# Joined column groups in a list scheduler, and a 64-row product run on 128 rows: a hybrid decoder layer on one Trainium2 core

## The chip, the core and the metric

The kernel runs on one core of one Trainium2 chip. The core has five engines that run their own queues of instructions: TensorE (in the profile PE for matmuls and PEld for the loads of their stationary operand), VectorE (DVE), ScalarE (ACT), GpSimd (POOL) and SyncE (SP), which here issues all DMAs. Matmuls read SBUF and write PSUM, which has eight banks. The metric is the device time of one execution in microseconds; the time of a kernel is the median of its runs.

## The reference, cut to what matters

One step of a decoder layer for two request groups: 2048 prompt tokens and 8 decode tokens, width 1024, all in float32. The layer has a parallel mixer (a Conformer convolution beside a gated DeltaNet with 4 heads), a cross-attention into 256 memory tokens, and a SwiGLU FFN of width 2816.

```python
def gated_delta_chunked(q, k, v, g, beta, s0):
    ...                                   # q, k, v, g, beta in chunks of 64 tokens
    lower = jnp.where(strict, jnp.einsum('nbhid,nbhjd->nbhij', kb, k) * decay, 0.0)
    a_mat = lower + jnp.eye(c, dtype=lower.dtype)
    u = lax.linalg.triangular_solve(a_mat, v * beta[..., None], left_side=True, lower=True, unit_diagonal=True)
    w = lax.linalg.triangular_solve(a_mat, kb * jnp.exp(gc)[..., None], left_side=True, lower=True, unit_diagonal=True)
    ...                                   # scan over the chunks with the state s

def memory_attend(h, mem_k, mem_v, w_mq, w_mo):
    q = (h @ w_mq).reshape(bsz, seq, MEM_HEADS, MEM_HD)
    s = jnp.einsum('blhd,bmhd->bhlm', q.astype(jnp.float32), mem_k.astype(jnp.float32)) * (MEM_HD ** -0.5)
    pr = jax.nn.softmax(s, axis=-1)
    o = jnp.einsum('bhlm,bmhd->blhd', pr, mem_v.astype(jnp.float32)).astype(h.dtype)
    return o.reshape(bsz, seq, MEM_HEADS * MEM_HD) @ w_mo

def decoder_layer(...):
    y, conv_buf, sc_buf, s = parallel_mixer(rms_norm(x, norm_mix), ...)
    x = x + y
    x = x + memory_attend(rms_norm(x, norm_mem_q), mem_k, mem_v, w_mq, w_mo)
    x = x + swiglu(rms_norm(x, norm_ffn), w_gate, w_up, w_down)
```

For the prompt, keys and values of the memory come from the memory tokens; each of the 8 decode rows has its own cached memory keys and values of 256 tokens.

## The kernel before, in words

The prompt is cut into four blocks of 512 tokens (`NB`, `TB`). For each pair of blocks the input projections run first; beside them run the convolution and the DeltaNet. Then come, block by block, the output projection, the memory attention and the FFN. The large products split each float32 operand into two parts of a shorter type and add three products (`three`), so that weights pass through a split on ACT and on DVE or POOL (tiles `w` out of `raw`). In the trace, `hd`, `glua` and `glub` are the input projections, `mkv`, `wk` and `vp` the memory's products, `rg` and `sc` the output projection and the memory attention, `fx`, `fy`, `fz` and `dn`, `dx`, `dy`, `dz` the FFN.

**The DeltaNet's inverse.** `dn_front` (lines 1795 to 1948) makes, for one head and one block of 512 tokens, the inverse of the lower triangular matrix; there are 4 x 4 = 16 such fronts. It works in four chunks of 128 tokens. `base_inverse` inverts the diagonal blocks of 16 rows on DVE and POOL; the result goes through DRAM (`zw`, `zt_`) into two tiles: `Tm`, and `W`, which first has 64 rows. Then blocks are joined, from 16 to 32 rows, from 32 to 64, and from 64 to 128. A step for `s` in (16, 32) is, in lines 1911 to 1932: four products of `lt` (or of its odd blocks, `lo`) and `Tm` into `pu1`; a multiplication with a mask on DVE into `u1`; four products of `W` and `u1` into `pu2`; an addition into `Tm` on DVE; four transposes of `Tm`, which ACT copies into a new `W` of 128 rows. In the step with s = 16 the second product runs on 64 rows (`W` has 64, and `u1[:n]` with n = 64), in the step with s = 32 on 128. Each of the four products is float32 and shows as two instructions, so a group of four shows as x8: `pu<-u,W 64*128` in the first step, `pu<-u,W 128*128` in the second. `u1` is one constant tile for all fronts; a front takes it with `held_l`, so one front uses it at a time.

`W`, `Tm` and most other working tiles come from one pool of 28 tiles (`t2`, `NT2`). Its users include the fronts' operands, the convolution's, the blocks of x, and the decode rows' operands.

**The decode rows' column groups.** `quad` (line 664) is a matmul whose stationary operand has at most 32 columns and whose result lies in PSUM rows 32j to 32j + 31. Four such products with j = 0 to 3 stand one after another in a loop at two places:

```python
                for (d, mc), vt in vts.items():                                       # line 2527, dec_attend
                    quad(po, 2 * d + mc, pbs[mc][:, (b + d) * 32 : (b + d + 1) * 32], vt, b == 0, b == DEC - 2)
        for j in range(4):                                                            # line 2433, dec_rows
            quad(at[0], j, h[:, k0 + j, :], wts[j], k0 == 0, k0 == 4)
```

The first is the product of probabilities and cached values of the decode rows (tile `podd`, moving operand `vtd`, 8 groups of four). The second is the decode rows' two projections `w_mq` and `w_mo` (tile `dr`, moving operand `raw`, 8 groups of four). Here too each product shows as two instructions.

**What sets the order.** The program is written down twice. First, generators ("lanes") and the main path issue operations in the order in which a simple clock finds them due; nothing is emitted yet, each goes onto a tape (`Tape.add`) with a modelled cost (`Tape.cost`). Then a list scheduler (`Tape.order`, lines 301 to 507) makes each engine's final order. `Tape.graph` finds which operations must come before which (`preds`). `Tape.keys` gives each a key: for PE its place on the tape; for other engines the smallest key among those that need its result or its tile next, but at most 300 (`LATER`) behind its own place. An engine that comes free takes, among the operations whose predecessors are done by the model's clock, the one with the smallest key. An operation whose tile isn't given yet also takes a buffer of its pool then; it may do so ahead of earlier users of the pool as long as the counts of live tiles leave room (`may`). Additions, subtractions and multiplications in SBUF may go to DVE or to POOL, whichever the scheduler finds better (`other`). So a change of a modelled cost, or one operation more, can change the order of everything behind it. The costs that bear on the change:

```python
            if args[1].dtype == F32 and m <= 32 and n >= 256:
                return n * 0.4492 + 15, False, None
```

and, for a fill on POOL, `40 + 0.85 * n` ns for n elements in a row.

Of the kernel before, what the change touches and what calls it, by code (L numbers as in the profile page):

```python
# [8 lines left out]
F32 = mybir.dt.float32  # L9
# [5 lines left out]
P = 128  # L15
# [5 lines left out]
NT = TB // P  # L21
# [133 lines left out]
class Tape:  # L155
# [10 lines left out]

    def __init__(self):
        self.ops, self.tag_of, self.bufs, self.psum = [], {}, {}, set()
        self.real, self.other, self.given = {}, {}, {}

    def pool(self, pool, bufs, psum=False):
        return TapePool(self, pool, bufs, psum)
# [16 lines left out]
    def cost(self, eng, op, args, kw, outs, ins):  # L189

        n = max(elems(a) for a in outs + ins) if ins else elems(outs[0])
        psum_in = any(a.name in self.psum for a in ins)
        if eng == "pe":
            m = elems(args[1])
            n = elems(args[2])
            if op == "transpose":
                return max(n, m) * 0.835 + 3, False, None
            if args[1].dtype == F32 and m <= 32 and n >= 256:
                return n * 0.4492 + 15, False, None
            if args[1].dtype == F32:  # L200
                return 2 * (max(max(m, 64) * 0.835, 2 * n * 0.4492) + 3), False, None
            return max(max(m, 64) * 0.835, (n if n >= 256 else 4 * n) * 0.4492) + 3, False, None
        if eng == "sp":
            size = 4
            for x in outs[0].shape:
                size *= x
            return max(size / 295.0, 90.0), False, None
        if eng == "act":
            ptr = len(ins) - 1
            return 0.834 * n + (50 if psum_in else 94) + 93 * ptr + (92 if "accum_out" in kw else 0), False, SETS.get(kw.get("func"))  # L210
        big = sum(a.name not in self.psum and elems(a) > 1 for a in ins)
        if eng == "dve":
            ptr = any(hasattr(kw.get(k), "shape") for k in ("scalar", "scalar1"))
            half = op in ("tensor_copy", "tensor_scalar") and not psum_in
            shared = big > 1 or (half and n > 2 and not any(a.name in self.psum for a in outs))
            return 68 + (61 if ptr else 0) + n * (6.2 if op == "reciprocal" else 0.525 if half else 1.042), shared, None
        if kw.get("op") == ALU.pow:
            return 280 + 180 * n, True, None
        if op in ("memset", "affine_select"):
            return 40 + 0.85 * n, False, None  # L220
        return 150 + n * (2.15 if op == "tensor_tensor" else 3.4), True, None

    def box(self, a):

# [20 lines left out]
    def graph(self):  # L245

        writes, reads, last_pe = {}, {}, {}
        preds, tiles = [], []
        over = lambda x, y: x[0] <= y[1] and y[0] <= x[1] and x[2] <= y[3] and y[2] <= x[3]
        inside = lambda x, y: y[0] <= x[0] and x[1] <= y[1] and y[2] <= x[2] and x[3] <= y[3]  # L250
        for n, (eng, op, _, args, _, outs, ins, _) in enumerate(self.ops):
            p = {}
            for a in ins:
                if a.name in self.tag_of:
                    b = self.box(a)
                    for k, x in writes.get(a.name, ()):
                        if over(b, x):
                            p[k] = 1
            for a in outs:
                if a.name in self.tag_of:  # L260
                    b = self.box(a)
                    for k, x in writes.get(a.name, ()):
                        if over(b, x):
                            p[k] = 1
                    for k, x in reads.get(a.name, ()):
                        if over(b, x):
                            p[k] = 1
                    if eng == "pe":
                        if a.name in last_pe:
                            p[last_pe[a.name]] = 1  # L270
                        last_pe[a.name] = n
            for a in outs:
                if a.name in self.tag_of:
                    b = self.box(a)
                    for d in (writes, reads):
                        d[a.name] = [(k, x) for k, x in d.get(a.name, ()) if not inside(x, b)]
                    writes[a.name].append((n, b))
            for a in ins:
                if a.name in self.tag_of:
                    reads.setdefault(a.name, []).append((n, self.box(a)))  # L280
            p.pop(n, None)
            preds.append(list(p))
            tiles.append(list(dict.fromkeys(a.name for a in outs + ins if a.name in self.tag_of)))
        return preds, tiles

    def keys(self, succs, line, first, tiles):


        N = len(self.ops)
        nxt = {}  # L290
        for tag, ts in line.items():
            for k, t in enumerate(ts[: -self.bufs[tag]]):
                nxt[t] = first[ts[k + self.bufs[tag]]]
        key = list(range(N))
        for n in range(N - 1, -1, -1):
            if self.ops[n][0] != "pe":
                after = [key[m] for m in succs[n]] + [key[nxt[t]] for t in tiles[n] if t in nxt and nxt[t] > n]
                key[n] = min([n + LATER, *after])
        return key

    def order(self):
# [336 lines left out]
def hybrid_step(ctx: ExitStack, tc: tile.TileContext, i: dict, o: list):  # L638
# [8 lines left out]
    def dma(out, in_, after=0.0):  # L647
        SP.dma_start(out=out, in_=in_)
        n = 4
        for x in out.shape:  # L650
            n *= x
        C.at["sp"] = max(C.at["sp"] + 60, C.when([in_]), after)
        C.at["dma"] = max(C.at["dma"], C.at["sp"] + 1100) + max(n / 360.0, 60.0)
        C.ready[out.name] = max(C.ready.get(out.name, 0.0), C.at["dma"] + 1650)
        C.used[in_.name] = max(C.used.get(in_.name, 0.0), C.at["dma"])

    def mm(out, lhsT, rhs, start, stop, skip=False):
        n = elems(rhs)
        four = lhsT.dtype == F32 or n < 256
        S.wait(max(C.when([lhsT, rhs]), C.ready.get("free " + out.name, 0.0) if start else 0.0))  # L660
        PE.matmul(out, lhsT, rhs, start=start, stop=stop, skip_group_check=skip)
        C.run("pe", 3 + max(n, 64) * (4 if four else 1) / 2.4, [lhsT, rhs], out, 90.0)
# [34 lines left out]
    def t2(name, shape=(P, TB), dt=F32):  # L697
        n = 1
        for x in shape[1:]:
            n *= x  # L700
        t = t2pool.tile([P, W2], dt, tag="t2", name=nm(name))
        live["t2"].add(t.name)
        assert len(live["t2"]) <= NT2, sorted(live["t2"])
        v = t[: shape[0], :n]
        if len(shape) == 3:
            v = v.rearrange("p (a b) -> p a b", a=shape[1])
        return v
# [34 lines left out]
    def const(name, shape, dt=F32):  # L742
        return cst.tile(list(shape), dt, tag=name, name=name)
# [1003 lines left out]
    def z_odd(z):  # L1747

        f = z.rearrange("a b -> (a b)").rearrange("(c x) -> c x", c=NT)
        return f[:, 0 : 64 * P].rearrange("c (r i) -> r c i", i=P)  # L1750
# [44 lines left out]
    def dn_front(h, b, sc, prev, out):  # L1795
# [96 lines left out]
        drop(bit, du)  # L1892
        held_x.pop()
        held_w.pop()
        W = t2("W", (64, NT, P))
        dma(W, z_odd(zw[z]))
        Tm = t2("Tm", (P, NT, P))
        dma(Tm, z_full(zt_[z]))
        yield lambda: prev is None or "done" in prev
# [11 lines left out]
        for s in LEV[:-1]:  # L1911
            n = nms[s].shape[0]
            yield ("ps", "s")
            pu = ps("pu1", shape=(n, NT, 64))
            for c in range(NT):
                mm(pu[:, c, :], (lo if n == 64 else lt)[:, c, :], left(Tm, s)[:, c], True, True)
            V.tensor_tensor(out=u1[:n], in0=pu, in1=bc(nms[s], 1, [n, NT, 64]), op=ALU.mult)
            yield u1
            yield ("ps", "s")
            pu = ps("pu2", shape=(P, NT, 64))  # L1920
            for c in range(NT):
                mm(pu[:, c, :], W[:, c, :], u1[:n, c, :], True, True)
            V.tensor_tensor(out=left(Tm, s), in0=pu.rearrange("p c (b s) -> p c b s", s=s), in1=left(Tm, s), op=ALU.add)
            yield Tm
            yield ("ps", "s")
            pt = ps("ptw", shape=(P, NT, P))
            for c in range(NT):
                transpose(pt[:, c, :], Tm[:, c, :], ident)
            drop(W)
            W = t2("W", (P, NT, P))  # L1930
            A.activation(out=W, in_=pt, func=AF.Copy)
            yield W
# [216 lines left out]
    drop(zt)  # L2149

    u1s = [const("u1", [P, NT, 64])]
    S.add(dec_start())
    fr_ = {(b, h): {} for b in range(NB) for h in range(H)}
    ch_ = {(b, h): {} for b in range(NB) for h in range(H)}
# [976 lines left out]
```

## Time and profile before

| what | us |
|---|---|
| median of 3 runs (lowest to highest) | 2936.22 (2935.59 to 2937.78) |
| the profiled execution's own time | 2932.24 |
| its span, first to last instruction | 2930.5 |
| PE busy in the span | 2890.9 |
| DVE busy | 2470.0 |
| ACT busy | 1452.0 |
| POOL busy | 754.0 |

The span is what the trace covers; the execution's own time also holds what lies around it. A row of a group of instructions reads: line, engine, operation, output <- inputs, shapes (for a matmul the active rows and columns of the stationary operand, then the moving operand), count; then busy time and mean length of one; then the engine's idle time ahead of them and what ended it. Line L515 is the place where the tape issues everything, so groups are told apart by tile names. A row of the timeline has the start, the time from start to end, and the merged instructions. A row by windows has the window, its length, and for each engine its busy time and number of instructions, then the granted TensorE clock, the share of the DMA engines and GB/s.

### The profile page before, as it was taken

The page shows a single profiled execution, that of the slowest core. Times are in us where ns is not written, and L with a number is a line of the kernel's source. Part 1 is how long each engine was busy: PE and PEld are TensorE (multiplying, and loading weights), DVE is VectorE, ACT ScalarE, POOL GpSimd, SP SyncE. Part 2 cuts the span into 40 slices and gives each one's busy share as a digit, 9 for nine tenths or more (in the row PEclk, how much of TensorE's full clock was granted, in tenths as well). Part 3 has the DMA queues.
Part 4 walks back from the last instruction along what each step waited for, and adds up shares of the span by engine and source line. Part 5 has one row for each costly group of instructions (what it writes and reads, how often), then busy time and mean ns, then how long its engine had stood idle before and what let it go on. Part 6 is the DMA issues. An engine that isn't in the chain of part 4 may idle for free.

```text
span 2930.5 us, 55769 instructions
## 1 busy us (share of the span) xinstructions
PE 2890.9 (99%) x19620; PEld 2598.0 (89%) x19620; DVE 2470.0 (84%) x5364; ACT 1452.0 (50%) x3034; POOL 754.0 (26%) x850
## 2 busy tenths in 40 slices
PE   9999999999999999999999999999999999999998
PEld 8999878888888887989888789999888999999998
DVE  8868988999978897978888877788867888888888
ACT  7544545555664445545454443344444444444444
POOL 3211342553313034613201810000542232410000
PEclk9999999999999999999999999999999999999999
DMA  6533435777774334866677767777636666666664
GB/s 222 155 97 105 128 115 162 228 247 258 225 243 124 119 102 133 261 192 201 213 259 251 246 217 246 232 232 238 201 102 207 210 214 199 209 230 197 214 209 131
DMA packets 363032, 569.40 MB, mean 194 GB/s; under 512 B 55840, under 2 KB 158560, under 8 KB 362736
## 3 DMA queue, kind: packets, MB, share of 16 engines
q1 hardware_dynamic: 362752, 565.84, 60.3%
q8 instruction: 155, 2.54, 0.3%
q14 instruction: 125, 1.02, 0.1%
HBM read 457.77 MB, written 108.51 MB: 193 GB/s over the span
## 4 chain that ended last, share of the span: by engine, by line
PE 51%; DVE 2%; DMA 2%; ACT 1%; issue 1%; POOL 0%; SPq 0%; POOLq 0%; DVEq 0%; ACTq 0%
PE fy L515 11%; PE fz L515 8%; PE fx L515 7%; PE rg L515 6%; PE dx L515 5%; PE dn L515 5%; PE dz L515 3%; PE sc L515 3%; PE dy L515 1%; DMA w<-sums 1%; DVE w L515 1%; PE pu L515 0%; PE podd L515 0%; DVE x L515 0%; PE pch L515 0%
## 5 line engine op out<-in xcount | busy, mean ns | idle before, releaser
L515 ACT ACTIVATE w<-raw 128x512 fp32r<-128x512 f32 (+1 forms) x1066 | 649.5, 619 | 888.9 <-issue 138.2
L515 DVE TENSOR_TENSOR w<-raw,w 128x512 fp32r<-128x512 f32 (+1 forms) x861 | 610.8, 713 | 161.5 <-ACT w L515 156.8
L515 PE MATMUL fy<-op,w 128*128 128x256 f32 (+1 forms) x3168 | 434.3, 282 | 0.1
L515 PEld LDWEIGHTS fy<-op,w 128*128 128x128 f32 x3168 | 399.1, 188 | 7.6 <-issue 1.8
L515 PE MATMUL hd<-hT,w 128*128 128x512 f32 (+2 forms) x1920 | 394.2, 356 | 1.0 <-DVE hT L515 0.5
L515 POOL TENSOR_TENSOR w<-raw,w 128x512 fp32r<-128x512 f32 (+1 forms) x205 | 282.5, 1382 | 341.7 <-ACT w L515 277.9
L515 DVE SCALAR_TENSOR_TENSOR cacc<-cu,cw,cacc 128x512 f32<-128x512 f32 x480 | 357.6, 745 | 9.2 <-ACT cacc L515 5.7
L515 PEld LDWEIGHTS hd<-hT,w 128*128 128x128 f32 x1920 | 302.6, 188 | 45.4 <-ACT w L515 1.2
L515 PE MATMUL fx<-op,w 128*128 128x256 f32 (+1 forms) x2112 | 297.3, 283 | 0.3
L515 PE MATMUL fz<-op,w 128*128 128x256 f32 (+1 forms) x2112 | 285.8, 283 | 1.8 <-DMA w<-sums 1.7
L515 PEld LDWEIGHTS fx<-op,w 128*128 128x128 f32 x2112 | 269.4, 189 | 8.3 <-ACT w L515 3.4
L515 PEld LDWEIGHTS fz<-op,w 128*128 128x128 f32 x2112 | 264.5, 188 | 9.0 <-issue 4.8
L515 PE MATMUL dx<-fo,w 128*128 128x256 f32 (+1 forms) x1344 | 197.8, 283 | 0.7 <-DVE x L515 0.6
L515 PE MATMUL rg<-pT,w 128*128 128x512 f32 x768 | 191.3, 400 | 2.1 <-ACT pr L515 0.9
L515 PE MATMUL dn<-ff,w 128*128 128x512 f32 (+2 forms) x960 | 192.0, 353 | 0.3 <-ACT ffs L515 0.2
L515 PE MATMUL sc<-w,hT 128*128 128x512 f32 x768 | 188.5, 399 | 3.6 <-ACT pr L515 3.6
L515 PE MATMUL rg<-catS,w 128*128 128x512 f32 (+2 forms) x960 | 186.2, 351 | 0.0
L515 PEld LDWEIGHTS dx<-fo,w 128*128 128x128 f32 x1344 | 174.7, 188 | 2.7 <-DVE x L515 1.3
L515 PEld LDWEIGHTS rg<-catS,w 128*128 128x128 f32 x960 | 154.6, 188 | 24.6
L515 PEld LDWEIGHTS sc<-w,hT 128*128 128x128 f32 x768 | 141.4, 188 | 36.8 <-ACT pr L515 5.9
L515 PEld LDWEIGHTS rg<-pT,w 128*128 128x128 f32 x768 | 140.5, 188 | 35.8 <-ACT pr L515 2.2
L515 PEld LDWEIGHTS dn<-ff,w 128*128 128x128 f32 x960 | 150.9, 188 | 22.0 <-DVE ffs L515 0.5
(421 smaller groups left out, 4836.6 us busy)
## 6 DMA issues: line engine op xcount, KB each, us to landing
w<-sums SPq DMA_DIRECT2D x222, 512.0 KB, 4.4
raw<-in_w_gate_dram SPq DMA_DIRECT2D x192, 256.0 KB, 3.5
sums<-w SPq DMA_DIRECT2D x66, 512.0 KB, 3.7
raw<-in_w_up_dram SPq DMA_DIRECT2D x118, 256.0 KB, 3.4
raw<-in_w_down_dram SPq DMA_DIRECT2D x224, 128.0 KB, 2.8
raw<-in_w_in_dram SPq DMA_DIRECT2D x96, 256.0 KB, 3.2
raw<-sums SPq DMA_DIRECT2D x74, 256.0 KB, 3.3
raw<-wk SPq DMA_DIRECT2D x64, 256.0 KB, 2.8
```

The costliest lines, as they stand in the source:

```text
L515: fn(*args, **kw)
```

## The change: two edits

**First edit, the list scheduler.** A new method `quarter` names a float32 matmul with at most 32 stationary columns and 256 or more moving ones. Its modelled cost goes from 0.4492 n + 15 to 0.4492 n + 38 ns. In `graph`, up to four such matmuls that follow one another on the tape's PE operations and write the same PSUM tile form a group: the predecessors of the second to fourth are added to those of the first, and the three are noted in `follow`. In `keys`, the key of those is lowered by the number of all operations, so that they come ahead of every other PE operation once the first has run.

**Second edit, the inverse.** `W` of the step from 16 to 32 gets 128 rows: the lower 64 are filled with zeros on POOL, the upper 64 are loaded as before. `u1` is filled with zeros once at the start. The second product of that step reads all 128 rows of `W` and of `u1`. What stands in the lower rows of `u1` from an earlier front is multiplied by zero.

```diff
--- before.py
+++ after.py
@@ -166,7 +166,7 @@
 
     def __init__(self):
         self.ops, self.tag_of, self.bufs, self.psum = [], {}, {}, set()
-        self.real, self.other, self.given = {}, {}, {}
+        self.real, self.other, self.given, self.follow = {}, {}, {}, set()
 
     def pool(self, pool, bufs, psum=False):
         return TapePool(self, pool, bufs, psum)
@@ -195,8 +195,8 @@
             n = elems(args[2])
             if op == "transpose":
                 return max(n, m) * 0.835 + 3, False, None
-            if args[1].dtype == F32 and m <= 32 and n >= 256:
-                return n * 0.4492 + 15, False, None
+            if self.quarter(op, args):
+                return n * 0.4492 + 38, False, None
             if args[1].dtype == F32:
                 return 2 * (max(max(m, 64) * 0.835, 2 * n * 0.4492) + 3), False, None
             return max(max(m, 64) * 0.835, (n if n >= 256 else 4 * n) * 0.4492) + 3, False, None
@@ -220,6 +220,10 @@
             return 40 + 0.85 * n, False, None
         return 150 + n * (2.15 if op == "tensor_tensor" else 3.4), True, None
 
+    def quarter(self, op, args):
+
+        return op == "matmul" and args[1].dtype == F32 and elems(args[1]) <= 32 and elems(args[2]) >= 256
+
     def box(self, a):
 
         if a.name in self.psum:
@@ -245,7 +249,7 @@
     def graph(self):
 
         writes, reads, last_pe = {}, {}, {}
-        preds, tiles = [], []
+        preds, tiles, group = [], [], []
         over = lambda x, y: x[0] <= y[1] and y[0] <= x[1] and x[2] <= y[3] and y[2] <= x[3]
         inside = lambda x, y: y[0] <= x[0] and x[1] <= y[1] and y[2] <= x[2] and x[3] <= y[3]
         for n, (eng, op, _, args, _, outs, ins, _) in enumerate(self.ops):
@@ -279,6 +283,15 @@
                 if a.name in self.tag_of:
                     reads.setdefault(a.name, []).append((n, self.box(a)))
             p.pop(n, None)
+            if eng == "pe" and self.quarter(op, args):
+                if group and group[0] == outs[0].name and len(group) < 5:
+                    preds[group[1]] = list(dict.fromkeys([*preds[group[1]], *(k for k in p if k < group[1])]))
+                    group.append(n)
+                    self.follow.add(n)
+                else:
+                    group = [outs[0].name, n]
+            elif eng == "pe":
+                group = []
             preds.append(list(p))
             tiles.append(list(dict.fromkeys(a.name for a in outs + ins if a.name in self.tag_of)))
         return preds, tiles
@@ -296,6 +309,8 @@
             if self.ops[n][0] != "pe":
                 after = [key[m] for m in succs[n]] + [key[nxt[t]] for t in tiles[n] if t in nxt and nxt[t] > n]
                 key[n] = min([n + LATER, *after])
+        for n in self.follow:
+            key[n] -= N
         return key
 
     def order(self):
@@ -1892,8 +1907,9 @@
         drop(bit, du)
         held_x.pop()
         held_w.pop()
-        W = t2("W", (64, NT, P))
-        dma(W, z_odd(zw[z]))
+        W = t2("W", (P, NT, P))
+        GS.memset(W[64:P], 0.0)
+        dma(W[0:64], z_odd(zw[z]))
         Tm = t2("Tm", (P, NT, P))
         dma(Tm, z_full(zt_[z]))
         yield lambda: prev is None or "done" in prev
@@ -1919,7 +1935,7 @@
             yield ("ps", "s")
             pu = ps("pu2", shape=(P, NT, 64))
             for c in range(NT):
-                mm(pu[:, c, :], W[:, c, :], u1[:n, c, :], True, True)
+                mm(pu[:, c, :], W[:, c, :], u1[:, c, :], True, True)
             V.tensor_tensor(out=left(Tm, s), in0=pu.rearrange("p c (b s) -> p c b s", s=s), in1=left(Tm, s), op=ALU.add)
             yield Tm
             yield ("ps", "s")
@@ -2149,6 +2165,7 @@
     drop(zt)
 
     u1s = [const("u1", [P, NT, 64])]
+    GS.memset(u1s[0], 0.0)
     S.add(dec_start())
     fr_ = {(b, h): {} for b in range(NB) for h in range(H)}
     ch_ = {(b, h): {} for b in range(NB) for h in range(H)}
```

## The prediction

> **What bounds the kernel now.** I read the page first: the busy times and the chain of work that ended last.
>
> ```profile
> span 2930.5 us, 55769 instructions
> PE 2890.9 (99%) x19620; PEld 2598.0 (89%) x19620; DVE 2470.0 (84%) x5364; ACT 1452.0 (50%) x3034; POOL 754.0 (26%) x850
> PE 51%; DVE 2%; DMA 2%; ACT 1%; issue 1%; POOL 0%; SPq 0%; POOLq 0%; DVEq 0%; ACTq 0%
> ```
>
> TensorE has 39.6 us without a matmul in 2930.5, and nearly all of the chain that could be followed is PE. So PE time that disappears should disappear from the end, unless the stage it lies in has another limit. For that I read the busy times by stage.
>
> ```profile
> core 0: us, PE busy (x) PEld busy (x) DVE busy (x) ACT busy (x) POOL busy (x), PEclk, DMA share, GB/s
> 140.00:455.00 315.00, 312.67 (x2021) 270.73 (x2019) 260.68 (x581) 149.43 (x339) 81.84 (x134) 1.00 0.37 112
> 455.00:640.00 185.00, 184.37 (x964) 152.18 (x963) 169.47 (x340) 104.29 (x225) 85.39 (x114) 1.00 0.67 215
> 640.00:700.00 60.00, 58.40 (x288) 46.47 (x287) 56.43 (x95) 29.23 (x50) 15.89 (x13) 0.97 0.75 250
> 700.00:1040.00 340.00, 329.55 (x2042) 283.62 (x2041) 286.80 (x576) 194.69 (x444) 83.80 (x100) 1.00 0.57 182
> 1040.00:1280.00 240.00, 235.37 (x1390) 203.22 (x1389) 209.67 (x395) 127.04 (x280) 113.08 (x110) 1.00 0.56 175
> 1280.00:1505.00 225.00, 223.47 (x1631) 204.73 (x1630) 188.37 (x376) 115.56 (x272) 46.68 (x55) 1.00 0.65 213
> 1505.00:1726.00 221.00, 217.19 (x1169) 180.40 (x1169) 193.62 (x315) 106.99 (x212) 82.38 (x62) 1.00 0.71 237
> 1726.00:1883.00 157.00, 155.82 (x1173) 138.30 (x1172) 111.58 (x264) 64.16 (x124) 4.67 (x5) 1.00 0.75 247
> 1883.00:2050.00 167.00, 166.65 (x1383) 160.91 (x1382) 140.38 (x355) 71.70 (x140) 0.74 (x1) 1.00 0.73 233
> 2050.00:2400.00 350.00, 349.06 (x2334) 319.11 (x2333) 280.10 (x598) 165.17 (x323) 123.32 (x102) 1.00 0.59 184
> ```
>
> The first number of a row is its length, the second PE's busy time. The stages of the inverse (140 to 1505) leave PE 2.33 + 0.63 + 1.60 + 10.45 + 4.63 + 1.53 = 21.2 us idle, half of it between 700 and 1040. In the stages of the column groups (1280 to 2050) PE idles 1.53, 3.81, 1.18 and 0.35 us, and 0.94 in the 350 us behind them. PE is the limit almost everywhere.
>
> But "busy" hides what this change touches: matmuls are pipelined, so a wait of the array to change its shape lies inside their durations. I therefore read starts, from the timeline of PE.
>
> **Part 1, the 64-row product.** Here is one 64-row product of the step from 16 to 32 (eight instructions for four chunks), and below it one 128-row product of the step from 32 to 64, both between 512-column matmuls.
>
> ```profile
> 142.94 1.09 PE L515 MATMUL hd<-hT,w 128*128 128x512 f32 x4
> 143.96 1.10 PE L515 MATMUL pu<-u,W 64*128 64x64 f32 x8
> 144.99 0.73 PE L515 MATMUL hd<-hT,w 128*128 128x512 f32 x2
> ```
>
> ```profile
> 315.73 0.94 PE L515 MATMUL glua<-hT,w 128*128 128x512 f32 x3
> 316.51 1.00 PE L515 MATMUL pu<-u,W 128*128 128x64 f32 x8
> 317.31 0.94 PE L515 MATMUL glua<-hT,w 128*128 128x512 f32 x3
> ```
>
> From its first start to the next matmul's start the 64-row group takes 144.99 - 143.96 = 1.03 us, the 128-row one 0.80: **0.23** more. Ahead of it, the last hd ends at 142.94 + 1.09 = 144.03, and the group starts 0.07 before that; the 128-row group starts 0.16 before the end of the glua (316.67): **0.09** more. Behind it, the second hd starts 0.73 - 0.39 = 0.34 after the first (0.39 is what one lasts); three glua in 0.94 give starts 0.23 and 0.32 apart: **0.02** more. Together 0.34 us, lost at the two borders and the first instruction, not in the products.
>
> ```profile
> L515 PE MATMUL pu<-u,W 64*128 64x64 f32 x128 | 17.6, 278 | 1.1 <-DVE u L515 1.1
> L515 PE MATMUL pu<-u,W 128*128 128x64 f32 x128 | 16.0, 268 | 0.0
> ```
>
> There are 128 / 8 = 16 such groups of each kind, so 16 x 0.34 = **5.4 us**. I take 128 rows here to cost what 128 rows cost one step later: same moving width of 64, same 128 weight columns. Bounds: 17.6 - 16.0 = 1.6 us, if only the busy time goes, and 5.4.
>
> Against padding speaks a rule of the Trainium skill, TensorEngine Tiling (Array Packing), "Theoretical Speedup": a contraction of 64 rows or fewer may run in two row tiles at once, up to twice as fast, and padding would give that away. Here the four chunks all use rows 0 to 63, and the two kinds take 17.6 and 16.0 us for as many instructions, so no pair ran at once and nothing is given away. By the rule this part would cost about 16 x 0.5 = 8 us in place of gaining 5.4.
>
> What part 1 adds: 16 fills of W's lower 64 rows and one of u1, all on POOL, and on each product a wait for POOL's fill. The nearest row is the fill of a whole tile.
>
> ```profile
> L515 POOL MEMSET dr<- x4: 518/525/527, 1279.6 to 1761.5; 128x512 f32 x4
> L515 ACT ACTIVATE dr<-dr x16: 587/590/593, 1504.3 to 2050.7; 8x512 f32<-8x512 f32 x16
> L515 SPq DMA_DIRECT2D W<-zw x16: 599/604/717, 128.0 to 1436.0; - x16
> ```
>
> A fill is 0.525 us, 16 make 8.4, in stages where POOL is busy 427 of 1365 us; what queues behind one on POOL is the subtraction of a weight split. I cost it at nothing, since POOL's idle two thirds hide it; without that cover it is at most 8.4 us. The wait itself is over long before: a fill has no input, so the list scheduler lets it run as soon as a tile is free. The dr fills show that: the first runs at 1279.6, and the tile is first written after it at 1504.3, 225 us on. W's load is issued at 128.0 and its first product stands at 143.96: 16 us. So W will be claimed earlier than now, out of 28 tiles. That is the danger of this change, and a rival below. u1 read on 128 rows adds no wait that ends late: its upper half was last written by the front before, which had to finish anyhow.
>
> **Part 2, the groups of four.** The column groups in 32 columns each (podd of the decode attention, dr of its projections) by windows of 2 us round each stretch of them; the second number is PE's busy time in these instructions, two per product, so x8 is a whole group, x4 and x2 are parts. Of the 14 windows of podd four rows and the sum, of the 10 of dr two and the sum.
>
> ```profile
> 1748.00:1750.00 2.00, 1.06 (x8) 0.16 (x8) 0.00 (x0) 1.00 0.68 190
> 1760.00:1762.00 2.00, 1.05 (x4) 0.14 (x4) 0.00 (x0) 1.00 1.08 399
> 1769.00:1771.00 2.00, 1.05 (x2) 0.14 (x2) 0.00 (x0) 1.00 1.00 320
> 1845.00:1847.00 2.00, 1.05 (x4) 0.14 (x4) 0.00 (x0) 1.00 1.03 408
> ...
> sum 28.00, PE 14.76 PEld 2.04 ACT 0.60; mean PE 1.05 PEld 0.15 ACT 0.04
> ```
>
> ```profile
> 1558.00:1560.00 2.00, 1.04 (x6) 1.00 0.04 13
> 1561.00:1563.00 2.00, 1.02 (x2) 1.00 0.63 216
> ...
> sum 20.00, PE 10.36; mean PE 1.04
> ```
>
> One product takes as long as four. podd has 64 instructions, so 8 groups, in 14.76 / 1.05 = 14 pieces; dr has 8 groups in 10.36 / 1.04 = 10 pieces. Eight pieces too many. What one costs, with its borders:
>
> ```profile
> 1772.03 0.51 PE L515 MATMUL fz<-op,w 128*128 128x256 f32 x3
> 1772.47 1.05 PE L515 MATMUL podd<-vtd,pb 128*32 128x512 f32 x2
> 1773.44 0.62 PE L515 MATMUL fy<-op,w 128*128 128x256 f32 x3
> ```
>
> From podd's start to fy's 0.97. Three fy behind it take 0.62 where three fz take 0.51: 0.11. Ahead, the last fz (0.28 long, ending at 1772.54) starts at 1772.26, 0.21 before podd; within the three, starts are (0.51 - 0.28) / 2 = 0.12 apart: 0.09. Together 1.17 us, and 8 x 1.17 = 9.4 us is the upper bound. The lower bound is 0: a part was put in where the planner had nothing earlier to run, and if each of these holes were real and 1.17 us long, a piece would only fill idle time. One is: behind the piece at 1845 PE waits a further microsecond for a weight. For the other seven the next matmul starts as soon as the array is free, and stages without such pieces idle little (0.94 in 350 us), so I let the holes be worth a quarter: 7 x 0.9 = **6.4 us**.
>
> Making the first wait for all four operands delays it by no more than the parts now lie apart (some 15 us at most), and PE has other products meanwhile; nothing else of PE is queued behind it, since the list puts the group in when it is ready. The new cost of a product (268 ns for 245 at 512 columns) shifts the plan's own clock by 23 ns each, under 2 us in all: worth nothing by itself.
>
> **The sum.** In the stage from 700 to 1040 PE already waits for others, and four of the 16 fronts lie there; I let a tenth of part 1 turn into such waits: 4.8 + 6.4 = 11.2 us. The profiled execution took 2932.24 with its span of 2930.5, which is 4.0 below the median of 2936.22; both should fall alike. Forecast **2925**, and about 2921 if profiled.
>
> **The rivals.** (a) The plan is laid anew, and only part comes through: the holes were real (part 2 brings 1 to 2 us) and half of part 1 turns into waits on DVE, which is busy 92% of the stage 455 to 640. For it: that load, and that a list moved by one fill orders everything behind it differently. Against it: 21.2 us of idle in 1365. It gives 2936.2 - 2.7 - 1.5 = 2932.
> (b) Slower, by W's early claim: 16 times one of 28 tiles is held for up to hundreds of us by zeros, and what needs a tile (loads of kT, x, the conv's operands) is issued later, so PE waits. It decides once all other tiles are live when W is claimed. For it: the dr fill at 1279.6. Against it: while that tile lay idle (1280 to 1505) PE idled 1.53 of 225 us. Price: were PE idle in all the inverse's stages as it is from 700 to 1040 (10.45 of 340, 3.1%), it would idle 41.9 in place of 21.2, 20.7 more; less the 11.2, 9.5 slower: 2946.
> (c) The change doesn't join the groups, because other PE work stands between the four on the tape; only part 1 comes: 2931. The four quad calls stand in one loop, which speaks against it; only a wait inside the loop of dr could let another lane in.
> (d) 64-row products overlap elsewhere in pairs and lose that by padding: 2936.2 + 8 - 6.4 = 2938. No row shows such a pair; the rule of packing above is what it would follow.
>
> **How the numbers follow.** Forecast 60% (own range 2917 to 2930), (a) 20%, (b) 13%, (c) 5%, (d) 2%. A change within 0.2% (5.9 us) can't be told from none. Faster by more than that (below 2930.3): the forecast, and a quarter of (a) and (c), as neither is exact: 0.65. Slower (over 2942.1): (b), 0.13. The rest, 0.22, is no change. Range: the low end takes both upper bounds, 2936.2 - 14.8, and 5 us for a plan that comes out better by a quarter of the 21.2 idle: 2916. The high end takes in (a), (c) and (d), and (b) up to a quarter of the 20.7, if nothing is gained: 2941.
>
> **What would show it.** Right: the pu rows with 64 rows are gone and x256 stand at 128 rows; 8 + 8 windows of column groups, all x8; PE busy down by 10 to 14 us, idle still near 40. Wrong: x2 or x4 pieces left (c); PE idle up by 10 us or more, with waits on DMA or DVE in the stages of the inverse (b); W's fill hundreds of us ahead of W's load with SP waiting for tiles.

## The result and the profile after

The changed kernel takes 2922.6 us in the median (2920.37 to 2923.71, 4 runs) beside 2937.0 us of the kernel before on the same chip: 14.4 us less, ratio 0.9947, 95% interval 0.9931 to 0.9962. Two later comparisons, on two other chips, gave 0.9939 (0.9927 to 0.9952) and 0.9943 (0.9930 to 0.9956). The forecast was 2925, the range 2916 to 2941.

The page of the changed kernel: span, busy times, the chain that ended last.

```profile
span 2918.7 us, 55833 instructions
PE 2880.8 (99%) x19620; PEld 2599.1 (89%) x19620; DVE 2477.8 (85%) x5383; ACT 1447.7 (50%) x3031; POOL 749.6 (26%) x848
PE 86%; DVE 7%; DMA 4%; issue 2%; ACT 1%; POOL 1%; SPq 0%; POOLq 0%; DVEq 0%; ACTq 0%
```

The profiled span is 11.8 us shorter. PE's busy time fell by 10.1 us, its idle time from 39.6 to 37.9. So the gain is PE work that is no longer there, as forecast.

The groups of instructions of the changed kernel, with busy time and mean length:

```profile
L530 PE MATMUL pu<-u,W 128*128 128x64 f32 x256 | 32.3, 268 | 0.0
L530 PE MATMUL podd<-vtd,pb 128*32 128x512 f32 x64 | 8.5, 604 | 0.0
```

No 64-row product is left, and podd's busy time fell from 14.76 to 8.5 us for the same 64 instructions. By windows of 2 us (length, busy time in these instructions alone, their number, clock, DMA share, GB/s), podd now stands in eight stretches, all x8; so does dr.

```profile
1719.00:1721.00 2.00, 1.07 (x8) 1.00 0.46 108
1753.00:1755.00 2.00, 1.06 (x8) 1.00 1.04 392
1852.00:1854.00 2.00, 1.06 (x8) 1.00 0.99 308
...
sum 16.00, PE 8.52; mean PE 1.07
```

```profile
1556.00:1558.00 2.00, 1.04 (x8) 1.00 0.00 0
...
sum 16.00, PE 8.36; mean PE 1.04
```

24 pieces have become 16. One product of the step from 16 to 32, in the timeline of the changed kernel (start, time from start to end, instructions):

```profile
143.74 1.31 PE L530 MATMUL hd<-hT,w 128*128 128x512 f32 x5
144.89 1.00 PE L530 MATMUL pu<-u,W 128*128 128x64 f32 x8
145.70 0.94 PE L530 MATMUL hd<-hT,w 128*128 128x512 f32 x3
```

It takes 0.81 us from start to next start where the 64-row one took 1.03, it starts 0.16 us before the last hd ends (143.74 + 1.31 - 144.89) where that one started 0.07 before, and the three hd behind it take 0.94 as behind the 128-row product of the other step in the prediction. The price of 128 rows is that of the other step, as assumed.

The forecast took this price from one pair of products. Over the whole trace all 16 64-row products of the kernel before take 1.03 us from their first start to the next matmul's. Of the 16 in the changed kernel 13 take 0.81, one stands in two parts (at 823 and 824.5 us), and two still take 1.03, at 1401.9 us and here:

```profile
397.60 1.10 PE L530 MATMUL pu<-u,W 128*128 128x64 f32 x8
398.63 0.43 PE L530 MATMUL peb<-dtmp,ones 8*128 8x64 f32 x2
```

The fill of W's lower rows and the load of its upper ones:

```profile
L530 POOL MEMSET W<- x16: 519/522/528, 14.1 to 1277.3; 64x512 f32 x16
L530 SPq DMA_DIRECT2D W<-zw x16: 599/604/750, 128.9 to 1434.0; - x16
```

The fills claim W's tile far ahead of its load, 115 us for the first, 157 for the last, and 28 to 204 for the others if fills and loads are paired in their order.

### The profile page after: what moved, and what is told of

Read it like the earlier page. It is cut to its first block, busy times and chain, and to the rows that moved or that the text cites. A ratio compares the mean times of both kernels' runs of the same rounds, so it can differ in the third digit from the quotient of the medians.

```text
span 2918.7 us, 55833 instructions
## 1 busy us (share of the span) xinstructions
PE 2880.8 (99%) x19620; PEld 2599.1 (89%) x19620; DVE 2477.8 (85%) x5383; ACT 1447.7 (50%) x3031; POOL 749.6 (26%) x848
## 3 DMA queue, kind: packets, MB, share of 16 engines
q14 instruction: 126, 1.03, 0.1%
## 4 chain that ended last, share of the span: by engine, by line
PE 86%; DVE 7%; DMA 4%; issue 2%; ACT 1%; POOL 1%; SPq 0%; POOLq 0%; DVEq 0%; ACTq 0%
PE hd L530 12%; PE fy L530 11%; PE rg L530 11%; PE fz L530 8%; PE fx L530 7%; PE dn L530 6%; PE dx L530 5%; PE sc L530 5%; PE glub L530 3%; PE glua L530 3%; PE dz L530 3%; PE pu L530 2%; DVE cacc L530 2%; PE mkv L530 1%; PE dy L530 1%
```

## Where the time went, in three stretches

The first and the last start of dr cut the span in three: the stretch of the inverse ahead of dr's first group, the stretch of all 16 column groups, and the rest. The kernel before and the changed one:

```profile
L515 PE MATMUL dr<-raw,hdn x32: 592/594/597, 1466.8 to 1561.6; 128*8 128x512 f32 x32
L515 PE MATMUL dr<-raw,hcat x32: 592/594/597, 1953.2 to 2048.2; 128*8 128x512 f32 x32
```

```profile
L530 PE MATMUL dr<-raw,hdn x32: 592/594/597, 1464.5 to 1556.5; 128*8 128x512 f32 x32
L530 PE MATMUL dr<-raw,hcat x32: 592/594/597, 1940.1 to 2035.4; 128*8 128x512 f32 x32
```

Ahead of the groups the change gained 1466.8 - 1464.5 = 2.3 us, in the stretch of the groups (2048.2 - 1466.8) - (2035.4 - 1464.5) = 581.4 - 570.9 = 10.5, and behind it (2930.5 - 2048.2) - (2918.7 - 2035.4) = 1.0 was lost. Read so, the inverse brought half of what was forecast and the groups two thirds more. My first theory (T in the expectations) was therefore: every piece costs its full 1.17 us, no hole pays for it; and the new order behind the early fills eats half of the inverse's gain, since TensorE's granted clock was 0.5 at 401, 814 and 919 us of this span, for 13.6 us together, and before only at 647, for 3.4.

## The experiments

All times are medians, each beside runs of the kernel before on the same chip.

| kernel | us | before | ratio, 95% interval |
|---|---|---|---|
| groups only | 2930.33 | 2937.66 | 0.9976 (0.9964 to 0.9988) |
| inverse only | 2935.37 | 2937.66 | 0.9991 (0.9981 to 1.0001) |
| fills only | 2937.38 | 2937.66 | 0.9995 (0.9986 to 1.0004) |
| late fill | 2979.35 | 2937.66 | 1.0140 (1.0123 to 1.0158) |
| changed, again | 2921.01 | 2939.81 | 0.9939 (0.9927 to 0.9952) |
| groups apart | 2969.28 | 2939.81 | 1.0104 (1.0090 to 1.0118) |
| zeros by load | 2941.67 | 2939.81 | 1.0003 (0.9992 to 1.0014) |
| W constant | 2947.83 | 2939.81 | 1.0029 (1.0019 to 1.0039) |
| groups only, again | 2929.89 | 2937.64 | 0.9968 (0.9956 to 0.9979) |
| inverse only, again | 2933.81 | 2937.64 | 0.9983 (0.9973 to 0.9993) |
| changed, third | 2922.30 | 2937.64 | 0.9943 (0.9930 to 0.9956) |
| old cost | 2923.55 | 2937.64 | 0.9950 (0.9936 to 0.9964) |

### The two edits alone

Groups only is the changed kernel with the inverse undone:

```diff
-        W = t2("W", (P, NT, P))
-        GS.memset(W[64:P], 0.0)
-        dma(W[0:64], z_odd(zw[z]))
+        W = t2("W", (64, NT, P))
+        dma(W, z_odd(zw[z]))
...
-                mm(pu[:, c, :], W[:, c, :], u1[:, c, :], True, True)
+                mm(pu[:, c, :], W[:, c, :], u1[:n, c, :], True, True)
...
-    GS.memset(u1s[0], 0.0)
```

> Only the first edit: groups joined, W with 64 rows as before. Theory T (every piece too many cost its full 1.17 us, the planner's holes were not real; and the new order behind the early fills ate half of the inverse's gain): 8 pieces fewer, 9 to 11 us faster than before, nothing gained ahead of 1450 us of the span. Rival R (the prediction's own split: the holes are worth a quarter, the inverse brings 4.8): 6.4 us faster.

Its first and last dr, in the first run and in the one that was repeated later:

```profile
L530 PE MATMUL dr<-raw,hdn x32: 592/594/597, 1472.7 to 1565.0; 128*8 128x512 f32 x32
L530 PE MATMUL dr<-raw,hcat x32: 592/594/597, 1949.1 to 2042.8; 128*8 128x512 f32 x32
```

```profile
L530 PE MATMUL dr<-raw,hdn x32: 592/594/597, 1473.7 to 1565.8; 128*8 128x512 f32 x32
L530 PE MATMUL dr<-raw,hcat x32: 592/594/597, 1948.8 to 2042.1; 128*8 128x512 f32 x32
```

The stretch of the groups takes 570.1 and 568.4 us where it took 581.4, 11.3 and 13.0 less, with 16 pieces. That speaks for theory T and against a quarter paid by holes. The surprise stands ahead of it: the first group starts at 1472.7 and 1473.7 where it started at 1466.8, although up to there PE's order is that of the kernel before to the last matmul. The profiled execution of the kernel before was thus a lucky one in that stretch, and a difference of two profiles tells no few microseconds there. Timed, it is 7.3 us, within an interval of 3.5 to 10.6: below the 9 to 11 that were expected, and the interval holds rival R's 6.4 as well. So the stretch decides here, not the time.

Inverse only is the kernel before with the second edit alone, fills only is inverse only with its product still on 64 rows:

```diff
-                mm(pu[:, c, :], W[:, c, :], u1[:, c, :], True, True)
+                mm(pu[:, c, :], W[:n, c, :], u1[:n, c, :], True, True)
```

> Only the second edit: W filled and read on 128 rows, groups as before (24 pieces). Theory T: about 2.5 us faster than before, and at the first column group (1465 us) PE stands as in the changed kernel, 2.4 us ahead of before; TensorE runs three windows of 3.4 us at half clock by then, or more, against one before. Rival R: 4.8 us faster. Rival F (the fills cost nothing, half clock is chance of the run): 5.4 us faster by the first column group in this run.

> The second edit's fills alone: W has 128 rows and its lower ones are filled as in the change, but the product reads 64 rows as before, so the zeros are of no use. Theory T: the fills' new order costs what is missing of the 5.4 us: about 3 us slower than before at the first column group and at the end. Rival R: 0 to 0.5 us slower.

Inverse only, the first time and repeated later, and fills only:

```profile
L515 PE MATMUL dr<-raw,hdn x32: 592/594/597, 1467.8 to 1562.3; 128*8 128x512 f32 x32
L515 PE MATMUL dr<-raw,hcat x32: 592/594/597, 1955.0 to 2052.5; 128*8 128x512 f32 x32
```

```profile
L515 PE MATMUL dr<-raw,hdn x32: 592/594/597, 1464.4 to 1558.9; 128*8 128x512 f32 x32
L515 PE MATMUL dr<-raw,hcat x32: 592/594/597, 1949.8 to 2046.8; 128*8 128x512 f32 x32
```

```profile
L515 PE MATMUL dr<-raw,hdn x32: 592/594/597, 1472.1 to 1566.6; 128*8 128x512 f32 x32
L515 PE MATMUL dr<-raw,hcat x32: 592/594/597, 1958.5 to 2055.1; 128*8 128x512 f32 x32
```

Inverse only is 2.3 us faster than before, within an interval of 5.6 faster to 0.3 slower, so its time holds theory T's 2.5 as well as rival R's 4.8. Fills only is not 3 us slower than before: the interval goes from 4.1 faster to 1.2 slower. The second half of theory T has fallen: the fills and the order behind them cost nothing that can be told. And its first group stands at 1472.1, as in groups only, whose order is the old one. Over all profiles at hand, the first dr starts at 1466.8, 1472.7 and 1473.7 with 64 rows and the old order (mean 1471.1), at 1472.1 with 64 rows and fills, and in the seven with 128 rows and fills (the changed kernel three times, inverse only twice, groups apart, old cost) at 1463.8 to 1467.8, mean 1465.3. That is **5.8 us** for part 1 against the mean of the old order, 6.8 against the one profile of the new order with 64 rows. The sum had said 5.4 and then taken a tenth off. The three profiles of the old order lie 6.9 us apart, and the earliest of them starts within the range of the seven, so a few us of this are uncertain. The 64-row products of fills only take 1.03 us like those of the kernel before, though their W has 128 rows: the price hangs on the rows that are read, not on the tile.

Timed, the inverse alone brings 2.3 and, when repeated, 3.8 us by medians, less than the traces show. The spread of runs is the reason why this can't be settled further: 29 runs of the kernel before on one chip go from 2932.3 to 2946.2, and with their mean granted clock (0.995 to 0.999) their time has a correlation of -0.90, 3.3 us for each 0.001. In the traces the clock is halved for 3.4 us or more behind some places where PE idles, though not in every profile of the same order. With fills these lie near 400, 815 and 920 us, in the old order near 647, 828 or 1264:

```profile
395.00:415.00 20.00, 20.00 (x107) 14.89 (x107) 19.12 (x50) 5.08 (x14) 6.04 (x18) 1.00 0.22 62
915.00:930.00 15.00, 15.00 (x89) 12.31 (x88) 8.88 (x27) 4.80 (x12) 6.73 (x15) 1.00 0.55 161
```

```profile
395.00:415.00 20.00, 18.59 (x90) 12.79 (x90) 18.12 (x48) 6.37 (x14) 9.27 (x22) 0.83 0.14 42
915.00:930.00 15.00, 12.50 (x62) 10.42 (x61) 12.89 (x20) 5.69 (x12) 10.67 (x10) 0.89 0.65 168
```

These are windows of the kernel before and of the changed one (length, busy PE, PEld, DVE, ACT, POOL, clock, DMA share, GB/s): the new order does idle there and is throttled behind it, as theory T said. Up to the first dr the half clock adds up to 17.1 us in fills only and to 3.4, 6.8 and 10.2 us in the three profiles of the old order; at half clock 17.1 us are worth 8.5 us of PE work, the others 1.7 to 5.1. Both orders reach the first dr at about the same time, so the new one must lose less elsewhere; where, these runs don't tell.

### Groups taken apart, and the modelled cost

Groups apart is the changed kernel with the three followers spread instead of joined:

```diff
-        self.real, self.other, self.given, self.follow = {}, {}, {}, set()
+        self.real, self.other, self.given, self.follow = {}, {}, {}, {}
...
-                    preds[group[1]] = list(dict.fromkeys([*preds[group[1]], *(k for k in p if k < group[1])]))
                     group.append(n)
-                    self.follow.add(n)
+                    self.follow[n] = len(group) - 2
...
         for n in self.follow:
-            key[n] -= N
+            key[n] += 24 * self.follow[n]
```

> The changed kernel, but the second to fourth product of each group get keys 24, 48 and 72 places later instead of earlier ones, and the groups are not joined: 54 pieces instead of 16. Theory T (a piece costs 1.17 us whatever is in it, and no hole pays for it): 38 x 1.17 = 44 us slower than the changed kernel. Rival R (a quarter of each is paid by holes): 33 us. Rival H (pieces fill holes): 0 to 10 us.

Its groups of instructions, and its first and last dr:

```profile
L529 PE MATMUL podd<-vtd,pb 128*32 128x512 f32 x64 | 28.3, 604 | 0.0
L529 PE MATMUL dr<-raw,hdn 128*8 128x512 f32 x32 | 15.4, 594 | 0.0
L529 PE MATMUL dr<-raw,hcat 128*8 128x512 f32 x32 | 12.3, 594 | 0.0
```

```profile
L529 PE MATMUL dr<-raw,hdn x32: 592/594/597, 1463.8 to 1571.1; 128*8 128x512 f32 x32
L529 PE MATMUL dr<-raw,hcat x32: 592/594/597, 1975.5 to 2082.1; 128*8 128x512 f32 x32
```

The busy times sum to 56.0 us, with 54 pieces. Each piece takes 0.96 to 0.99 us from its start to the next matmul's, whether it holds one, two or three products; in the kernel before, each of the 24 takes 0.96 to 1.00, but for the one at 1845 us with its wait of 1.04. The stretch of the groups takes 618.3 us, 47.4 more than in the changed kernel, and the whole is 48.3 us slower than the changed kernel beside it (2969.28 to 2921.01): **1.27 us** for each of 38 pieces. By the two stretches it is 1.25. A piece costs a little more than 1.17, and nothing shows a hole that pays for it.

Old cost is the changed kernel with `n * 0.4492 + 15` again for a column product.

> The changed kernel with the old modelled cost of a column product (0.4492 n + 15): groups joined, 16 pieces; the order of PE differs in 59 of 18512 places. Theory: the cost is worth nothing by itself, within 3 us of the changed kernel. Rival: it is part of the gain, more than 4 us slower than the changed kernel.

It is 1.3 us slower than the changed kernel beside it, and both intervals overlap almost wholly: the modelled cost is worth nothing that can be told, as the theory said.

### No early claim: three other ways to the zeros, or to the tile

Late fill lets ACT write the zeros, out of Tm, so that the fill can't run ahead of Tm's load:

```diff
-        GS.memset(W[64:P], 0.0)
         dma(W[0:64], z_odd(zw[z]))
         Tm = t2("Tm", (P, NT, P))
         dma(Tm, z_full(zt_[z]))
+        A.activation(out=W[64:P], in_=Tm[64:P], func=AF.Copy, scale=0.0)
```

> The changed kernel, but W's lower rows are zeroed by ACT, as zero times Tm's lower rows, so that the fill has an input and cannot claim W's tile ahead of its load. Theory T: if the early claim is what costs the 3 us, 2 to 4 us faster than the changed kernel (about 2919 to 2920), with PE 5 us ahead of before at the first column group. Rival O (any new order of the list costs or gains a few us, whatever the claim): anywhere within 4 us of the changed kernel, with the loss or gain standing at other places than the fills. Rival R: as the changed kernel.

Zeros by load lets W's load bring all 128 rows from a larger DRAM tile:

```diff
-        GS.memset(W[64:P], 0.0)
-        dma(W[0:64], z_odd(zw[z]))
+        dma(W, z_odd(zw[z]))
...
-        dma(z_odd_diag(zw[z]), w16[1:32:2, 0:256].rearrange("p (j i) -> p j i", i=16))
+        for c in range(NT):
+            dma(z_odd_diag(zw[z])[c], w16[1 + 8 * c : 8 + 8 * c : 2, 0:256].rearrange("p (j i) -> p j i", i=16))
...
-    zw = [dram.tile([16, 2080], F32, tag=f"zw{k}", name=f"zw{k}") for k in range(NZ)]
+    zw = [dram.tile([32, 2080], F32, tag=f"zw{k}", name=f"zw{k}") for k in range(NZ)]
...
```

The views of this DRAM tile and its filling with zeros at the start are fitted to its new size, which the diff leaves out.

> The changed kernel, but W's lower rows come as zeros from DRAM with its load (the load moves 256 instead of 128 KB, the store ahead of it is four DMAs instead of one), so there is no fill and no early claim of W's tile. Theory T (the early claim's order costs 3 us, through half clock near 400 and 815 us): no half clock at these two places, PE 5 us ahead of before at the first column group, 2 to 4 us faster than the changed kernel. Rival O (the list's new order decides, whatever makes it): no relation, 20 us faster to 40 us slower than the changed kernel.

W constant keeps one tile for it, filled once:

```diff
-NT2 = 28
+NT2 = 27
...
-    held_x, held_w, held_l = [], [], []
+    held_x, held_w, held_l, held_16 = [], [], [], []
...
-        W = t2("W", (P, NT, P))
-        GS.memset(W[64:P], 0.0)
+        yield lambda: not held_16
+        held_16.append(1)
+        W = w64
         dma(W[0:64], z_odd(zw[z]))
...
-            drop(W)
+            if s == 16:
+                held_16.pop()
+            else:
+                drop(W)
...
+    w64 = const("w64", [P, NT, P])
+    GS.memset(w64, 0.0)
```

> The changed kernel, but W of the first step is one constant tile, its lower rows filled once; to make room the working pool has 27 tiles instead of 28, and one front at a time holds the constant. Theory T: no fills, no early claims, 0 to 4 us faster than the changed kernel, unless the lost tile costs it. Rival O: no relation, 20 us faster to 40 us slower than the changed kernel.

All three were meant to save the claim and are slower than the changed kernel: the late fill by 1.0140 / 0.9943, 58 us, by the two ratios to before, and the other two by 20.7 and 26.8 us beside it. Theory T has no room for that. Rival O of zeros by load and W constant (20 us faster to 40 slower) holds. For the late fill neither theory holds: its own rival O had allowed 4 us. Zeros by load and W constant reach the first dr at 1465.5 and 1463.2 us, as early as the changed kernel, but by then PE has run 64 and 110 matmuls fewer than there, so their stretches can't be set beside the others. Their clock is halved at other places than 400, 815 and 920 us (582, 770, 831 and 975; 376, 591, 850 and 1219), by the first dr for 17.1 us in each: half clock stands there without early claims, too. In the late fill PE idles 76 us where it idled 38, by the page and by the waits of PE (in total, times, longest):

```profile
PE 2899.3 (97%) x19620; PEld 2614.9 (88%) x19620; DVE 2476.2 (83%) x5393; ACT 1460.5 (49%) x3047; POOL 732.0 (25%) x822
```

```profile
PE pu L530 <- DMA Tm<-zt: 11.3, 4, 6.4
PE dn L530 <- ACT ffs L530: 6.8, 3, 5.8
PE pod L530 <- ACT osc L530: 4.4, 2, 3.4
```

A large part of the loss is one cluster of waits from 1026 us on, first 3.4 us for `osc` from ACT and then 6.4 for Tm's load; from 1030 us the clock is at half for 37.5 us. Why the list comes out so in these three, these runs don't tell. Each rewrite also changes something besides the claim: an operation more on ACT between load and product, a larger load with four stores ahead of it, one working tile less. So they don't price the claim; that it costs nothing rests on fills only.

### Do the parts add?

On three chips the parts made 7 and 2 us and the whole 14 to 18, so all three were run once more beside each other.

> The changed kernel again, beside the others on one chip. If the two edits only add, it is 9.6 us faster than before (7.3 for the groups alone and 2.3 for the inverse alone); as first measured, 14.

> The first edit alone once more, now beside the second alone and both on one chip, since the parts (7 and 2 us) fell short of the whole (14 to 18 us) on different chips. Theory A (the parts add; the rest was scatter by half clock): 9 to 11 us faster than before. Theory I (the edits help each other): 7 us again.

> The second edit alone once more. Theory A: 3 to 5 us faster than before, and with the groups' time as much as the whole. Theory I: 2 us again.

> The changed kernel beside its parts. Theory A: as much as the two parts together, 13 to 15 us faster than before. Theory I: 14 to 18, at least 4 more than the parts.

The second run of the changed kernel brought 17.9 us (14.1 to 21.5), not the 9.6 of the first parts. By the ratios of the last comparison the groups bring 9.4 us (6.2 to 12.9), the inverse 5.0 (2.1 to 7.9), and the whole 16.7 (12.9 to 20.6): 14.4 and 16.7 agree within their intervals. By plain medians it is 7.8, 3.8 and 15.3, and the whole is 3.8 us more than its parts, close to the 4 of theory I. So theory A fits best, but the times don't exclude that the edits help each other by some us.

The stretches speak for theory A more clearly. Inverse only reaches the first dr as early as the changed kernel (1467.8 and 1464.4 us against 1464.5, 1465.1 and 1466.8), and groups only needs as long for the stretch of the groups (570.1 and 568.4 us against 570.9, 569.3 and 568.9). Each edit does in its own stretch alone what it does there in the whole.

## Why the prediction came right, step by step

- **PE is the limit, so PE work that goes leaves the end.** Right: 10.1 us less PE busy, 11.8 us less span, and 37.9 us idle in place of 39.6.
- **Part 1, 16 x 0.34 = 5.4 us.** Right. The products look as assumed, and the stretch ahead of the column groups is 5.8 us shorter by the means of ten profiles, give or take a few. If only the 13 products at 0.81 gain the 0.34, that makes 4.4 us, close to the 4.8 that went into the sum. But the sum had let a tenth turn into waits, and what is missing here are the three products that gain less or nothing. The sum was made against a profile that was lucky there by some 4 us (1466.8, mean of its order 1471.1); it did no harm, since the forecast took the terms off the median.
- **The fills at nothing.** Right: fills only is within 0.9986 to 1.0004 of before. The danger that I named, the tile claimed early, does happen (115 to 157 us ahead at the two ends) and costs nothing that can be told.
- **Part 2, eight pieces less.** Right in number, 24 to 16 (rival c is out). The price of a piece was right and a little low, 1.17 against 1.25 to 1.27. What failed is the discount, "so I let the holes be worth a quarter: 7 x 0.9 = 6.4 us": no hole is seen to pay for anything. (7 x 0.9 is 6.3, and a tenth off 5.4 leaves 4.9 in place of 4.8; the sum of 11.2 stands.) The stretch of the groups takes 581.4, 584.7, 582.4 and 583.0 us in the four profiles with 24 pieces and 568.4 to 571.9 in the six with 16 that run as many matmuls in it; without the three rewrites of the fill, that is. By the means it is 13.0 us less: 10.4 of PE busy (576.9 to 566.5) and 2.6 of PE idle (5.9 to 3.4). Eight pieces at 1.17 are 9.4 of the busy time. Another 1.3 by the means is half clock: in three of the four profiles the clock is halved for 3.4 us near 1675 us, in none of the six. Some 2 us of the idle time are a wait of the score products for the probabilities at that place, which stands in the kernels with 24 pieces and not in those with 16. In the kernel before and in inverse only, repeated:

```profile
PE sc L515 <- ACT pr L515: 3.6, 3, 2.0
```

```profile
PE sc L515 <- ACT pr L515: 3.0, 2, 2.0
```

and in the changed kernel:

```profile
PE sc L530 <- ACT pr L530: 1.0, 1, 1.0
```

I had no term for the wait or for the half clock behind it. Groups apart, with 54 pieces, has a wait for the probabilities at that place too (2.3 us); whether the joined groups or only the changed order took it away is not shown.
- **The sum.** 4.8 + 6.4 = 11.2 was forecast; 14.4 was measured first, and 17.9 and 16.7 later. The size that was off is the second term, 6.4 for about 13. By the stretches the change makes 5.8 + 13.0 us, and about one is lost behind the groups (883.6 us from the last dr to the end by the mean of the four, 884.8 of the six, single profiles from 882.3 to 886.0). That the first measurement lies only 2.4 us from the forecast is in part luck: it is the smallest of three gains.
- **The other rivals.** (a) is out, since PE's idle time did not rise and part 2 brought more than its 1 to 2 us. (b) is out by fills only. (d), which gave padding a loss of 8 us, is out by inverse only: it is not slower than before but 2.3 and 3.8 us faster by medians. That inverse only is 2.0 us faster than fills only in the same comparison is within the noise of both.
- **The range.** Its upper end took the price of a new order from the idle time of one stage, and of these 20.7 us only a quarter. Three small edits of the list cost 21 to 58 us against the changed kernel. The range was right for this change; the price in it of a new order was too low.

## What to carry to other kernels

Where PE is busy 99% of the time, its busy time still hides the borders between differently shaped matmuls; read starts, from the matmul ahead to the second one behind, and count the borders. A piece that is put in by a list scheduler "where there is a hole" is to be priced in full unless the trace shows PE waiting right behind it. Under a list scheduler, test each edit alone and repeat the kernel before often: here one profile differed by 7 us from another at the same matmul of the same order, and three rewrites of one fill cost more than the whole change had gained.

## What the runs showed of the hardware that I had not expected

TensorE's clock can be granted at half behind a cluster of short gaps. In the changed kernel it is halved for 6.8 us from 401 us on; the window of the 14 us ahead of that:

```profile
386.50:400.50 14.00, 12.07 (x83) 9.64 (x81) 13.80 (x37) 9.82 (x15) 5.92 (x10) 1.00 0.31 98
```

PE idles 1.9 us there, in gaps of which the longest is 0.64 us. The Trainium skill, in TensorE: Matmul & The Clock Gate, "Why this matters for your kernels", advises against gaps over about 3 us between bursts of matmuls; here the clock is halved behind much shorter ones. The two other profiles of the changed kernel are halved there too, for 3.4 and 6.8 us. But such gaps needn't do it: old cost idles as much in the 14 us ahead, its longest gap is 0.64 us as well, and its clock stays full.

```profile
387.00:401.00 14.00, 12.09 (x82) 9.54 (x80) 13.83 (x37) 9.81 (x15) 5.94 (x10) 1.00 0.32 98
401.00:415.00 14.00, 13.13 (x61) 9.15 (x61) 13.72 (x37) 1.63 (x5) 7.29 (x18) 1.00 0.07 19
```

What decides between the two is not shown. Over the 29 runs of one program a mean clock lower by 0.001 goes with 3.3 us more. By an estimate, 0.001 of 2937 us is 5.9 us at half clock, worth 2.9 us of PE work, so the halving would account for most of the spread of runs.
